# A two-layer diffusion block: mixers and the later units of a front are emitted in step with the expert gathers, with their VectorE work kept behind the dots

## The chip, the cores and the metric

The kernel runs on one core of a Trainium2 chip. The metric is the device time of one execution in microseconds (us); the median of three runs of the kernel before is 2957.38 us (2956.25 to 2957.57). The engines are TensorE (PE: matmuls; PEld: its weight loads), VectorE (DVE), ScalarE (ACT), GpSimd (POOL) and SyncE (SP). SP issues the plain transfers of the program in one queue, POOL the gathers.

## The reference, cut to what matters

Two streams of 256 tokens, the latent `x` and the context `ctx`, go through two layers. A layer has a mixer (attention and a bidirectional delta rule, the latent one reading the context's keys and states) and an expert layer (PEER): per token 8 heads pick 16 experts each out of 16384, by the top 16 of two lists of 128 keys and the top 16 of their sums. The context's expert layer is left out in the last layer.

```
x = x + g1 * mixer(rmsnorm(x, norm1_w) * (1 + sc1) + sh1, ctx...)
h = rmsnorm(x, norm2_w) * (1 + sc2) + sh2
q = (h @ wq);  s = q . subkeys;  sv, si = top_k(s, 16)          # the front
top_s, pos = top_k(sv[0] + sv[1], 16);  gate = softmax(top_s)
u = peer_u[expert];  act = gelu(sum(u * h))                    # a gather and a dot
x = x + g2 * sum(gate * act * peer_v[expert])
```

## The kernel before

A tile framework records instructions in the order in which the Python code emits them and then orders them itself: a scheduler plays the program with its own cost model and places each instruction on its engine when, in that play, it can run; emission order is its priority. On the chip each engine then runs its list strictly in order. Pools of tiles (`bufs` buffers a tag) make an instruction wait until a buffer's last reader is done.

The stages follow in `build` (L1063): the context's mixer of layer 0, `peer_start` and `peer_end` for it (expert layer 1, 0 by stream and layer), the latent mixer of layer 0 and its expert layer (0, 0), the context's mixer of layer 1 (keys and states only), the latent mixer of layer 1, and its expert layer (0, 1). The mixer of (0, 0) reads nothing of the context's expert layer, so the scheduler may run it beside those gathers; likewise the mixer of (1, 1) reads the context's result and runs beside the gathers of (0, 0). The latent mixer of layer 1 needs the last result of (0, 0) and has no gathers beside it.

An expert layer begins with its front (`peer_front`, L801): the norm to `h2`, transposes to `h2T`, eight heads of `wq` products (`ps_pq`), scores `sc`, and then `topk` (L888) in units. `CUTS` cuts the eight heads of the first 128 tokens (t=0) in units of 1, 2, 2 and 3 heads and those of the second 128 (t=1) in two units of 4. A unit ends with its list of indices `idx`. With `hl` (expert layers (1, 0) and (0, 1)) the front's products are made of three products of float32r halves (`product`, L150; a weight is split by ScalarE into `whi` and by VectorE into `wlo`, L127 and L128); without it each is one f32 product (L154).

`experts` (L1000) yields once per gather, 256 to an expert layer, 768 in all: POOL issues an indirect DMA of 1 MB into a buffer `G` (`gather`, L984); VectorE makes the dot `junk<-G,h2r` (L1024, with a small instruction that reads the sum); ScalarE makes `dg` (L1028, L1029); TensorE multiplies the second half of `G` into `acc` (L1033), which frees the buffer for a later gather. `h2r` are four copies of rows of `h2`, written by DMAs on SP (`replicated`), with one buffer each, so those for t=1 wait for the last dots of t=0. There are 7 gather buffers, 8 from the second half of expert layer (1, 0) on, and again 7 and then 14 in the last expert layer. `peer_start` emits the front's unit i+1, then the dots of unit i; the units of t=1 are emitted in step with the last unit of t=0, and `peer_end` runs the rest.

Of the kernel before, what the change touches and what calls it, by code (L numbers as in the profile page):

```python
# [38 lines left out]

QUADS = 4  # L40
QP = P // QUADS
QD = D // QUADS
GATHERS = 7
MORE_GATHERS = (1, 7)
# [7 lines left out]
def _blk(i, n):  # L52
    return slice(i * n, (i + 1) * n)
# [39 lines left out]

class Net:
    def __init__(self, tc, ap, out):
        self.tc, self.nc, self.ap, self.out = tc, tc.nc, ap, out

# [13 lines left out]
    def rsqrt(self, pool, x, n, mul, eps, tag):  # L111

        v = self.nc.vector
# [12 lines left out]
    def split(self, x, hi, lo):  # L126
        self.nc.scalar.copy(hi, x)  # L127
        self.nc.vector.tensor_tensor(lo, x, hi, op=ALU.subtract)  # L128
# [12 lines left out]
    def weight(self, name, l, i, hl, pool=None):  # L141
# [5 lines left out]
        lo = self.hlpool.tile([P, D], F32R, tag="wlo", name="wlo", bufs=self.lo_bufs)  # L147
# [29 lines left out]
    def late_constants(self, pool):  # L177
# [7 lines left out]
        with self.pool("clev_f") as cf:  # L185
            lf = cf.tile([P, 14, P], F32, name="clevf")
            nc.sync.dma_start(lf, ap["k_levels"].rearrange("m p n -> p m n"))
            nc.vector.tensor_copy(lv, lf)
# [40 lines left out]
    def modulation(self, l, pr, chunks):  # L229
# [7 lines left out]
        for n in chunks:  # L237
# [15 lines left out]
            nc.vector.tensor_tensor(  # L253
# [5 lines left out]
    def scale_columns(self, pr, i):  # L259

        for s in range(2):
            self.nc.vector.scalar_tensor_tensor(
# [21 lines left out]
    def rms_scale(self, pool, ss, n, tag):  # L284

        tot = pool.tile([P, n], F32, tag=tag + "_tot", name="tot")
        self.nc.vector.tensor_tensor(tot, ss[:, 0:n], ss[:, n : 2 * n], op=ALU.add)
        return self.rsqrt(pool, tot, n, 1.0 / D, EPS, tag)

    def norm1(self, pool, s, pr, hl):  # L290
# [3 lines left out]
        with self.pool(f"n1{s}") as pn:  # L294
            ss = pn.tile([P, 2 * NT], F32, name="n1ss")
            xn = []
            for t in range(NT):
# [4 lines left out]
                nc.vector.tensor_scalar_mul(xt, x[t], rs)  # L302
                xn.append(xt)
            for g in range(KB // 2):
# [4 lines left out]
                for j in range(2):  # L309
                    kb = 2 * g + j  # L310
                    a, b = pr["acol"][:, s, 0, kb : kb + 1], pr["mod"][:, s, kb : kb + 1]
                    if hl:
# [3 lines left out]
                        nc.vector.tensor_copy(hi, f)  # L316
                        nc.vector.tensor_tensor(lo, f, hi, op=ALU.subtract)
                    elif j == 0:
                        nc.vector.tensor_scalar(h[0][:, kb, :], ps[:, _blk(j, T)], a, b, op0=ALU.mult, op1=ALU.add)
# [25 lines left out]
    def attn_proj(self, pool, h, s, l, need_q, hl):  # L345
# [8 lines left out]
        def use_kv(t, ps):  # L354
            nc.scalar.copy(_flat(raw[t][:, NH:, :]), ps[:, :256])
            nc.vector.tensor_copy(_flat(vv[:, t]), ps[:, 256:])
# [6 lines left out]
    def attention(self, pool, raw, vv, pr, s, need_q, mixT):  # L363

        nc, v = self.nc, self.nc.vector
# [80 lines left out]
    def dn_project(self, pool, h, pr, l, blocks, qk, vtok, hl):  # L446

        nc, v = self.nc, self.nc.vector
# [21 lines left out]
    def dn_gates(self, pool, h, pr, l, g, beta, hl):  # L470

        nc, v = self.nc, self.nc.vector
# [3 lines left out]
        if hl:  # L476
            hi = self.hlpool.tile([P, D], F32R, tag="whi", name="whi")
            lo = self.hlpool.tile([P, D], F32R, tag="wlo", name="wlo", bufs=self.lo_bufs)
# [39 lines left out]
    def dn_norm(self, pool, qk, first, ktok, qT, kT):  # L518

        nc, v = self.nc, self.nc.vector  # L520
# [28 lines left out]
    def dn_chunk(self, pool, dn, t, d, it):  # L549
# [6 lines left out]
        nc, v = self.nc, self.nc.vector  # L556
# [89 lines left out]
    def dn_step(self, pool, it, vtok, d, S, O, first_o, new_S):  # L646

        nc, v = self.nc, self.nc.vector
# [53 lines left out]
    def dn_output(self, pool, O, gate, pr, mixT):  # L702
        nc, v = self.nc, self.nc.vector
# [19 lines left out]
    def mixer(self, s, l, pr, big, filler=(), rate=1, late_mods=(), late_consts=None):  # L723

        nc, v, hl = self.nc, self.nc.vector, big
# [75 lines left out]
    def peer_front(self, s, l, pr, hl, cuts):  # L801

        nc, v, ap = self.nc, self.nc.vector, self.ap
# [3 lines left out]
        with ExitStack() as st:  # L807
            pt = st.enter_context(self.pool("pt" + nm))
            hT = self.operand(pt, [P, KB, T], "h2T", hl)
            with self.pool("pn" + nm) as pn:  # L810
                A2 = self.broadcast_rows(pn, pr["acol"][:, s, 1, :], "A2")
                SH2 = self.broadcast_rows(pn, pr["mod"][:, s, 24:32], "SH2")

                h2.append(self.gbuffer()[:, :D] if hl else pt.tile([P, D], F32, name="h2"))
# [466 lines left out]
```

## Time and profile before

| | |
|---|---|
| median of three runs | 2957.38 us |
| the profiled execution | 2954.79 us |
| its span | 2952.7 us |
| TensorE busy | 1891.7 us (64%) |
| VectorE busy | 1866.0 us (63%) |
| ScalarE busy | 1094.0 us (37%) |
| GpSimd busy | 915.8 us (31%) |
| DMA, mean over the span | 326 GB/s |

No engine is near its full span. The stages have to be looked at one by one: by the granted clock, the DMA share (mean busy share of the 16 DMA engines) and the rate of the dots. A dot is counted in the views as two instructions of L1024. Dot k below is the k-th of the 768; dots 1 to 256 belong to expert layer (1, 0), 257 to 512 to (0, 0) and 513 to 768 to (0, 1).

### The profile page before, as it was taken

The page shows a single profiled execution, that of the slowest core. Times are in us where ns is not written, and L with a number is a line of the kernel's source. Part 1 is how long each engine was busy: PE and PEld are TensorE (multiplying, and loading weights), DVE is VectorE, ACT ScalarE, POOL GpSimd, SP SyncE. Part 2 cuts the span into 40 slices and gives each one's busy share as a digit, 9 for nine tenths or more (in the row PEclk, how much of TensorE's full clock was granted, in tenths as well). Part 3 has the DMA queues.
Part 4 walks back from the last instruction along what each step waited for, and adds up shares of the span by engine and source line. Part 5 has one row for each costly group of instructions (what it writes and reads, how often), then busy time and mean ns, then how long its engine had stood idle before and what let it go on. Part 6 is the DMA issues. An engine that isn't in the chain of part 4 may idle for free. (4 is left out here: it accounts for less than half of the span.)

```text
span 2952.7 us, 38689 instructions
## 1 busy us (share of the span) xinstructions
PE 1891.7 (64%) x13184; PEld 1085.0 (37%) x13184; DVE 1866.0 (63%) x4942; ACT 1094.0 (37%) x2609; POOL 915.8 (31%) x772
## 2 busy tenths in 40 slices
PE   7998836876888834458774444488988344444444
PEld 5876713533654611124550000077767110010001
DVE  5854798756775895446774444487557964455454
ACT  4533434745442432236442222254234322222222
POOL 0000234233343334332443444200002444435552
PEclk9999956997989955568985555599989555555555
DMA  7234899988999989999999999831358899999997
GB/s 277 100 121 168 290 342 354 348 359 326 339 370 374 416 303 394 394 418 367 366 352 372 420 420 419 359 115 44 115 193 319 315 378 419 420 375 420 420 419 308
DMA packets 163314, 961.64 MB, mean 326 GB/s; under 512 B 20784, under 2 KB 28336, under 8 KB 64816
## 3 DMA queue, kind: packets, MB, share of 16 engines
q0 software_dynamic: 110592, 805.36, 68.7%
q1 hardware_dynamic: 52528, 153.83, 15.0%
q8 instruction: 106, 1.74, 0.2%
q14 instruction: 88, 0.72, 0.1%
HBM read 945.48 MB, written 1.05 MB: 321 GB/s over the span
## 5 line engine op out<-in xcount | busy, mean ns | idle before, releaser
L988 POOL DMA_INDIRECT G<-in_peer_uv,idx x768 | 915.6, 1192 | 2001.7 <-PE acc L1033 762.3
L1024 DVE CUSTOM_DVE_ANT_0 junk<-G,h2r 128x1024 bf16<-128x1024 f32 x768 | 937.1, 1220 | 576.1 <-DMA G<-in_peer_uv,idx 554.6
L1033 PE MATMUL acc<-G,dg 128*32 128x256 f32 x6144 | 720.1, 558 | 889.8 <-ACT dg L1029 886.9
L1028 ACT ACTIVATE dg<-cident,act 128x32 f32<-128x32 f32 x768 | 246.7, 321 | 1158.9 <-DVE act L1024 1133.6
L1033 PEld LDWEIGHTS acc<-G,dg 128*32 128x32 f32 x6144 | 147.8, 130 | 1401.8 <-ACT dg L1029 1353.4
L1029 ACT ACTIVATE dg<-dg,pgate 128x32 f32<-128x32 f32 x768 | 246.6, 321 | 23.3
L128 DVE TENSOR_TENSOR wlo<-w,whi 128x1024 fp32r<-128x1024 f32 (+1 forms) x98 | 117.5, 1202 | 53.3 <-ACT whi L127 52.9
L127 ACT CAST whi<-w 128x1024 fp32r<-128x1024 f32 (+1 forms) x98 | 100.9, 1032 | 123.4 <-PE ps_pr L158 36.4
L621 PE MATMUL ps_P<-M,B 128*128 128x128 f32 x768 | 116.3, 299 | 33.7 <-DVE M L630 21.5
L621 PEld LDWEIGHTS ps_P<-M,B 128*128 128x128 f32 x768 | 101.3, 205 | 67.8 <-issue 35.0
L628 DVE COPY_PREDICATED X<-clev,ps_X 128x512 f32<-128x512 int8 x96 | 69.8, 727 | 73.6 <-PE ps_X L627 73.6
L627 PE MATMUL ps_X<-X,Pm 128*128 128x128 f32 x768 | 104.1, 281 | 1.5 <-ACT Pm L623 1.4
L623 ACT COPY Pm<-ps_P 128x512 f32<-128x512 f32 x96 | 56.2, 586 | 125.0 <-PE ps_P L621 124.2
L627 PEld LDWEIGHTS ps_X<-X,Pm 128*128 128x128 f32 x768 | 94.3, 194 | 16.5 <-issue 8.8
L244 PE MATMUL ps_ada<-w,silc 128*32 128x512 f32 x384 | 78.0, 666 | 10.2 <-DMA w<-in_ada_t 10.0
L462 DVE SCALAR_TENSOR_TENSOR cy<-craw,cw,cy 128x256 f32<-128x256 f32 x176 | 81.3, 481 | 2.0
L154 PE MATMUL ps_dn<-hT,w 128*128 128x256 f32 x320 | 81.2, 409 | 0.0
L1028 ACT ACT_TABLE_LOAD x57 | 73.1, 1283 | 14.3 <-DVE act L1024 13.3
L158 PE MATMUL ps_pq<-h2T_hi,wlo 128*128 128x256 f32 x256 | 75.4, 294 | 4.5 <-DVE wlo L128 4.4
L156 PE MATMUL ps_pq<-h2T_hi,whi 128*128 128x256 f32 x256 | 74.6, 291 | 0.6 <-ACT whi L127 0.6
L157 PE MATMUL ps_pq<-h2T_lo,whi 128*128 128x256 f32 x256 | 74.1, 290 | 0.0
L154 PEld LDWEIGHTS ps_dn<-hT,w 128*128 128x128 f32 x320 | 63.9, 206 | 16.5 <-issue 7.4
(316 smaller groups left out, 3081.2 us busy)
## 6 DMA issues: line engine op xcount, KB each, us to landing
w<-in_ada_t SPq DMA_DIRECT2D x96, 512.0 KB, 5.5
w<-in_wq_t SPq DMA_DIRECT2D x48, 512.0 KB, 5.3
w<-in_in_dn SPq DMA_DIRECT2D x44, 512.0 KB, 6.9
w<-in_in_rows SPq DMA_DIRECT2D x40, 512.0 KB, 4.0
w<-in_out_t SPq DMA_DIRECT2D x24, 512.0 KB, 5.3
G<-in_peer_uv,idx POOLq DMA_INDIRECT x768, 14.2
h2r<-h SPq DMA_DIRECT2D x64, 128.0 KB, 10.4
h2r<-G SPq DMA_DIRECT2D x32, 128.0 KB, 2.4
```

Of the source, the lines that this page charges most:

```text
L127: self.nc.scalar.copy(hi, x)
L128: self.nc.vector.tensor_tensor(lo, x, hi, op=ALU.subtract)
L154: self.nc.tensor.matmul(out, lhs[0], rhs[0], start=first, stop=last)
L244: nc.tensor.matmul(ps[_blk(g, 32), :], self.silc[:, kb, :], w[:, _blk(k, CW)], start=(kb < 4), stop=(kb >= 4))
L462: v.scalar_tensor_tensor(y, raw[:, k : k + T], cw[:, blk, k : k + 1], y, op0=ALU.mult, op1=ALU.add)
L621: nc.tensor.matmul(pp[:, _blk(h, P)], B[:, h, :], M[:, h, :], start=True, stop=True)
L627: nc.tensor.matmul(xp[:, _blk(h, P)], Pm[:, h, :], X[:, h, :], start=True, stop=True)
L988: self.nc.gpsimd.indirect_dma_start(out=G, out_offset=None, in_=self.ap[f"peer_uv{l}"], in_offset=bass.IndirectOffsetOnAxis(ap=idx, axis=0))
L1024: v.tensor_tensor_reduce(self.junk, G[:, :D], un["h2r"][j], scale=1.0, scalar=0.0, op0=ALU.mult, op1=ALU.add, accum_out=a)
L1028: nc.scalar.activation(dg, self.ident4, AF.Gelu, scale=a)
L1029: nc.scalar.mul(dg, dg, un["gate"][:, m, j : j + 1])
L1033: nc.tensor.matmul(self.acc[_blk((j + q) % QUADS, QP), _blk(q, QD)], dg, G[:, D + QD * q : D + QD * q + QD], start=(un["first"] and m == 0 ...
```

## The change

A class `Paced` stands in for the VectorE engine everywhere but in the dots' own units. It holds a queue of `experts` generators. While a pace is set, each VectorE instruction that a mixer or a front emits adds 0.1 + elements/960 to a counter, and at each full `pace` the next gather, dot and product of the queue are emitted right there. With `pin`, the VectorE instruction emitted after such a step is kept behind it in program order (`keep_in_program_order`), so the scheduler can't move it ahead of that dot.

`peer` replaces `peer_start` and `peer_end`: the first two units of a front are emitted without steps, the later ones at a pace of 1.0; pinned in (0, 0) and (0, 1), not in (1, 0). What is left in the queue is emitted in step with the mixer that follows, at a pace of 1.0 (mixer (0, 0)) and 0.7 (mixer (1, 1)), pinned, or drained at the end. All fronts use f32 products, and `h2` of t=0 has a tile of its own instead of a gather buffer. There are 8 gather buffers from the start of each group, and 14 for what is left after the last front.

```
-GATHERS = 7
-MORE_GATHERS = (1, 7)
+FRONT_PACE = 1.0
+MIXER_PACE = (1.0, 0.7)
+GATHERS = 8
+MORE_GATHERS = 6
...
+class Paced:
+    def step(self):
+        while self.queue:
+            self.inside = True
+            done = next(self.queue[0], self) is self
+            self.inside = False
+            if not done:
+                return True
+            self.queue.pop(0)
+        return False
...
+        def paced(*args, **kw):
+            ins = op(*args, **kw)
+            if self.inside or not self.pace:
+                return ins
+            if self.behind and self.pin:
+                self.tc.keep_in_program_order(ins)
+            self.behind = False
+            sizes = [math.prod(a.shape[1:]) for a in args if hasattr(a, "shape")]
+            self.due += 0.1 + max(sizes) / 960.0
+            while self.due >= self.pace:
+                self.due -= self.pace
+                self.behind |= self.step()
+            return ins
...
-    def peer_front(self, s, l, pr, hl, cuts):
+    def peer_front(self, s, l, pr, cuts):
...
-                    w = self.weight("wq_t", l, 2 * h + j, hl)
+                    (w,) = self.weight("wq_t", l, 2 * h + j, False)
...
+    def peer(self, s, l, pr, pin):
         cuts = [[(sum(u[:i]), n) for i, n in enumerate(u)] for u in CUTS]
+        self.dve.set()
+        for i, un in enumerate(self.peer_front(s, l, pr, cuts)):
+            self.dve.queue.append(self.experts(s, l, un))
+            if i == 1:
+                self.dve.set(FRONT_PACE, pin)
+        self.dve.set()
...
+                    self.peer(1, 0, prs[0], False)
                 with ExitStack() as st:
                     psums(st, 3, 3)
+                    self.dve.set(MIXER_PACE[0], True)
                     self.mixer(0, 0, prs[0], False)
-                    units = self.peer_start(0, 0, prs[0], False)
-                self.peer_end(0, 0, units)
+                    self.peer(0, 0, prs[0], True)
                 with ExitStack() as st:
                     psums(st, 3, 3)
                     _run(params[1])
+                    self.dve.set(MIXER_PACE[1], True)
                     _run(mods(1, range(0, 4), 0))
                     self.mixer(1, 1, prs[1], False)
+                    self.dve.set()
+                self.dve.drain()
```

How the built programs differ is read from the order of the instructions on an engine. All engines' lists are the same up to the end of the context's first mixer. First place: VectorE in the first unit of the first front, (1, 0), from the splits of its weights to the one-hot products `oh`; before:

```order
L128 TENSOR_TENSOR wlo<-w,whi 128x1024 x3
L910 MAX sv<-sc_2709 128x8 x2
...
L128 TENSOR_TENSOR wlo<-w,whi 128x1024
L910 MAX top<-cand 128x8
...
L963 TENSOR_TENSOR ge<-top 128x16
L128 TENSOR_TENSOR wlo<-w,whi 128x1024
L932 TENSOR_SCALAR r<-pos 128x16
...
L950 TENSOR_TENSOR oh<-ab,ciota 128x256 x2
L128 TENSOR_TENSOR wlo<-w,whi 128x1024
```

And now, where every VectorE instruction has the wrapper's line, L131:

```order
L131 CAST ciota<-ciotaf 128x1024
L131 MAX sv<-sc_2701 128x8 x2
...
L131 MAX top<-cand 128x8
...
L131 TENSOR_TENSOR ge<-top 128x16
L131 TENSOR_SCALAR r<-pos 128x16
...
L131 TENSOR_TENSOR oh<-ab,ciota 128x256 x2
```

The splits of the weights are gone from between the steps of the unit. Second place: VectorE where the mixer of (0, 0) makes its first normalised row `xn`. Before, it follows dot 45, and the fronts' last units have just passed:

```order
L981 CAST idx<-ps_ig 32x64
...
L1024 ISA junk,act<-G,h2r 128x1024
L1024 ISA act 128x1
L120 TENSOR_TENSOR n_t<-n_y 128x1
...
L302 TENSOR_SCALAR xn_6670<-res_x_79,n_y 128x1024
...
L1024 ISA junk,act<-G,h2r 128x1024
L1024 ISA act 128x1
L302 TENSOR_SCALAR xn_6692<-res_x_80,n_y 128x1024
```

Now it follows dot 85, and between dots 42 and 85 VectorE has nothing but dots:

```order
L131 ISA junk,act<-G,h2r 128x1024
L131 ISA act 128x1
L131 ISA junk,act<-G,h2r 128x1024
L131 ISA act 128x1
L131 SCALAR_TENSOR_TENSOR n_t<-n_t,n_a 128x1
L131 SCALAR_TENSOR_TENSOR n_y<-n_t,n_y 128x1
L131 TENSOR_SCALAR xn_4555<-res_x_79,n_y 128x1024
```

So this mixer starts 40 dots later. Its last row of `h` comes after dot 228 instead of 177. Of the next front's index lists `idx`, the four of t=0 come after dots 239 to 263 instead of 188 to 221, and the two of t=1 after dots 277 and 303 instead of 256 and 272 (where the maxima and one-hots for them were through by dot 228). The mixer of (1, 1) has its scan (`ps_P`) beside dots 360 to 412 instead of 328 to 360. Third place: TensorE where the front of (0, 0) begins, after its transposes `ps_h`. Before, products of the front and of the dots alternate:

```order
L154 MATMUL ps_pq<-h2T,w 128x256 x12
L1033 MATMUL acc<-G,dg 32x256 x4
L154 MATMUL ps_pq<-h2T,w 128x256 x4
L1033 MATMUL acc<-G,dg 32x256 x4
L154 MATMUL ps_pq<-h2T,w 128x256 x13
...
L154 MATMUL ps_pq<-h2T,w 128x256 x3
L1033 MATMUL acc<-G,dg 32x256 x16
L854 MATMUL ps_sc<-skT,pqT 128x128 x4
```

Now they stand in blocks (four products of L1084 are one dot's):

```order
L899 MATMUL ps_pq<-h2T,w 128x256 x32
L1084 MATMUL acc<-G,dg 32x256 x28
L907 MATMUL ps_sc<-skT,pqT 128x128 x4
L1084 MATMUL acc<-G,dg 32x256 x4
L899 MATMUL ps_pq<-h2T,w 128x256 x28
L1024 MATMUL ps_ig<-ig,crep 128x32 x4
L907 MATMUL ps_sc<-skT,pqT 128x128 x8
L899 MATMUL ps_pq<-h2T,w 128x256 x4
L1084 MATMUL acc<-G,dg 32x256 x28
```

So up to 32 products of the front are ahead of the products that free the buffers of seven dots. In the attention of mixer (0, 0) the dots move a little as well: it has eight passes of a maximum `am`, an exponent on ScalarE and a reciprocal `asm` on VectorE, and a dot stands between the last two in five of the eight, where it was one. After dot 256, at the change of expert layers, 65 VectorE instructions of the front now stand before dot 257, where there were 8. ScalarE's list has 133 loads of function tables where it had 127.

## Rows read from the trace of the kernel before

**Rows 1.** The page, DMA queues: packets, MB, time as share of 16 engines' span.

```profile
q0 software_dynamic: 110592, 805.36, 68.7%
```

**Rows 2.** Stretches, L1024 alone: length, VectorE busy (x instructions), PE clock, DMA share, GB/s.

```profile
334.00:485.00 151.00, 52.75 (x87) 0.64 0.91 343
485.00:935.00 450.00, 163.73 (x268) 0.88 0.92 353
935.00:1095.00 160.00, 53.63 (x87) 0.79 0.93 370
1095.00:1190.00 95.00, 43.27 (x72) 0.57 1.00 377
1337.00:1543.00 206.00, 78.47 (x129) 0.90 0.94 357
1671.00:1871.00 200.00, 98.54 (x160) 0.50 1.01 419
2245.00:2392.00 147.00, 52.38 (x85) 0.63 0.90 339
```

**Rows 3.** Stretches, all: length, PE, PEld, DVE, ACT, POOL, clock, DMA share, GB/s.

```profile
0.00:334.00 334.00, 291.76 (x1926) 236.10 (x1927) 205.84 (x539) 140.15 (x249) 0.27 (x5) 0.94 0.50 171
334.00:485.00 151.00, 76.28 (x574) 42.06 (x576) 138.70 (x620) 59.39 (x156) 65.81 (x49) 0.64 0.91 343
485.00:935.00 450.00, 357.54 (x2361) 216.53 (x2353) 303.37 (x663) 223.43 (x484) 162.93 (x137) 0.88 0.92 353
935.00:1095.00 160.00, 109.16 (x711) 71.41 (x710) 135.88 (x629) 57.26 (x156) 49.73 (x44) 0.79 0.93 370
2245.00:2392.00 147.00, 75.61 (x563) 41.41 (x562) 137.43 (x610) 57.68 (x147) 61.93 (x49) 0.63 0.90 339
```

**Rows 4.** Waits of POOL, 485 to 935 us: us in total, times, longest.

```profile
POOL G L988 <- PE acc L1033: 137.7, 57, 12.2
```

**Rows 5.** Waits of DVE in the same stretch.

```profile
DVE asm L429 <- ACT ap L428: 16.8, 8, 2.4
DVE junk L1024 <- DMA G<-in_peer_uv,idx: 15.1, 9, 2.6
```

**Rows 6.** Timeline of DVE, attention of mixer (0, 0): start, us, instruction [idle before].

```profile
700.72 0.15 DVE L427 TENSOR_SCALAR am<-am 128x1 f32<-128x1 f32 x1
703.28 0.16 DVE L429 RECIPROCAL asm<-asm 128x1 f32<-128x1 f32 x1 [2.42 <-ACT ap L428]
703.40 1.23 DVE L1024 CUSTOM_DVE_ANT_0 junk<-G,h2r 128x1024 bf16<-128x1024 f32 x1
```

**Rows 7.** Timeline of DVE, first unit of the first front: its first and last step.

```profile
313.54 0.48 DVE L910 MAX8 sv<-sc 128x8 f32<-128x128 f32 x2
...
326.35 0.18 DVE L960 SCALAR_TENSOR_TENSOR ig<-oh 128x16 f32<-128x16 bf16 x1
```

**Rows 8.** Groups of DVE, 313.5 to 330.5 us: busy us, mean ns | idle before.

```profile
L128 DVE TENSOR_TENSOR wlo<-w,whi 128x1024 fp32r<-128x1024 f32 x6 | 7.4, 1225 | 3.4 <-ACT whi L127 3.4
```

**Rows 9.** Timeline of PE, first front: float32r halves, three products to a block.

```profile
302.84 0.28 PE L158 MATMUL ps_pq<-h2T_hi,wlo 128*128 128x256 f32 x1
...
303.20 0.28 PE L158 MATMUL ps_pq<-h2T_hi,wlo 128*128 128x256 f32 x1
```

**Rows 10.** Timeline of PE, front of (0, 0): f32, one product to a block.

```profile
937.61 5.35 PE L154 MATMUL ps_pq<-h2T,w 128*128 128x256 f32 x24
```

**Rows 11.** Timeline of POOL: the first gather of (1, 0).

```profile
333.93 1.08 POOL L988 DMA_INDIRECT G<-in_peer_uv,idx  x1 [333.48 <-DVE sv L910]
```

**Rows 12.** The same view: the first gather of (0, 1).

```profile
2244.96 0.94 POOL L988 DMA_INDIRECT G<-in_peer_uv,idx  x1 [348.66 <-DVE sv L910]
```

**Rows 13.** Timeline of DVE: between dot 256 and dot 257.

```profile
1178.90 0.08 DVE L1024 DVE_READ_ACCUMULATOR2_ANT act<- 128x1 f32 x1
...
1190.74 1.22 DVE L1024 CUSTOM_DVE_ANT_0 junk<-G,h2r 128x1024 bf16<-128x1024 f32 x1
```

**Rows 14.** The page, groups: busy us, mean ns | idle before.

```profile
L1028 ACT ACT_TABLE_LOAD x57 | 73.1, 1283 | 14.3 <-DVE act L1024 13.3
```

More of the change, by code (lines that the diff above doesn't have):

```diff
@@ L91, in _zip, with __init__, set, drain @@
         yield
+class Paced:
+    def __init__(self, tc):
+        self.tc, self.vector = tc, tc.nc.vector
+        self.queue, self.pace, self.pin = [], 0.0, False
+        self.due, self.behind, self.inside = 0.0, False, False
+    def set(self, pace=0.0, pin=False):
+        self.pace, self.pin, self.due = pace, pin, 0.0
+    def step(self):
[7 more added lines that the diff above has]
+        return False
+    def drain(self):
+        while self.step():
+            pass
+    def __getattr__(self, name):
+        op = getattr(self.vector, name)
+        def paced(*args, **kw):
[11 more added lines that the diff above has]
+            return ins
+        return paced
 class Net:
@@ L843, in head @@
                 for j in range(2):
-                    w = self.weight("wq_t", l, 2 * h + j, hl)
+                    (w,) = self.weight("wq_t", l, 2 * h + j, False)
                     for kb in range(KB):
-                        self.product(
-                            ps[:, _blk(j, T)], [a[:, _blk(kb, P)] for a in w], [a[:, kb, :] for a in hT], kb == 0, kb == KB - 1
+                        nc.tensor.matmul(
+                            ps[:, _blk(j, T)], w[:, _blk(kb, P)], hT[:, kb, :], start=(kb == 0), stop=(kb == KB - 1)
                         )
@@ L858, in head @@
                     nc.scalar.copy(_flat(sc[t][:, 2 * h : 2 * h + 2, :]), ps[:, _blk(t, T)])
-            for h0, n in cuts[0]:
+            for i, (h0, n) in enumerate(cuts[0]):
                 tk = self.topk(pool, sc[0], h0, n)
@@ L1058, in experts @@
                 v.tensor_tensor(xs, xs, out, op=ALU.add)
-    def peer_start(self, s, l, pr, hl):
+    def peer(self, s, l, pr, pin):
         cuts = [[(sum(u[:i]), n) for i, n in enumerate(u)] for u in CUTS]
-        front = self.peer_front(s, l, pr, hl, cuts)
-        n0 = len(cuts[0])
-        units = [next(front)]
-        def rest():
-            for un in front:
-                if un is not None:
-                    units.append(un)
-                for _ in range(5):
-                    yield
-        for i in range(n0):
-            if i + 1 < n0:
-                units.append(next(front))
-            _run(self.experts(s, l, units[i]), rest() if i == n0 - 1 else None)
-        return units
-    def peer_end(self, s, l, units):
-        for un in units[len(CUTS[0]) :]:
-            _run(self.experts(s, l, un))
+        self.dve.set()
[4 more added lines that the diff above has]
+        self.dve.set()
     def build(self):
@@ L1173, in build @@
                     psums(st, 3, 3)
-                    self.hlpool = pool("hl3", 2, st)
-                    self.lo_bufs = 2
-                    units = self.peer_start(0, 1, prs[1], True)
-                self.more_gathers(ga, MORE_GATHERS[1])
-                self.peer_end(0, 1, units)
+                    self.peer(0, 1, prs[1], True)
+                self.more_gathers(ga, MORE_GATHERS)
+                self.dve.drain()
             for t in range(NT):
```

64 lines of the change are left out of this document (28 added, 36 removed).

## The prediction

> **What bounds the kernel now.** I read the page's table of queues first. The gathers move 805 MB, 768 of 1 MB [rows 1]. Then I cut the span at its stages and counted dots, two instructions to a dot [rows 2]. Where no front or mixer runs beside them (1671 to 1871 us) 80 dots take 200 us, 2.50 us each, at a DMA share of 1.01: there the transfers are the limit. 768 of them make 1920 us. The first stage (334 us) and the latent mixer of layer 1 have no gathers beside them and are not touched before their last few us. What the change can win is the difference between 2.50 us and the pace beside fronts and mixers [rows 2]: 3.47 us a dot in the first front (43.5 dots in 151 us), 3.36 in mixer (0, 0) (134 in 450), 3.68 in the front of (0, 0) (43.5 in 160), 3.19 in mixer (1, 1) (64.5 in 206), 3.46 in the last front (42.5 in 147).
>
> Two causes are to be seen. In the fronts VectorE is the limit: busy 138.7 of 151, 135.9 of 160 and 137.4 of 147 us [rows 3]. In mixer (0, 0) VectorE is busy 303 of 450 us, yet a dot waits for its gather for 15 us in all [rows 5], while POOL waits 138 us for the products that free a buffer [rows 4]. So the dots stand in line behind a mixer's instruction that waits for another engine. One case: a reciprocal waits 2.42 us for the exponent, and the dot behind it, ready or not, starts only then [rows 6].
>
> Part of that difference is no loss: the mixers' weights use the same DMA engines. In the first 334 us a share of 0.50 moved 171 GB/s [rows 3], that is 167 us for 57 MB, some 1.5 us for a weight of 0.52 MB. The 48 weights of mixer (0, 0) and the front behind it are thus worth 73 us. From 485 to 1190 us there are 213.5 dots [rows 2]: 534 + 73 = 607 us of transfers in 705 us.
>
> **The change part by part.**
>
> *Fronts in f32.* A block of 256 columns starts every 0.36 us with halves (302.84 to 303.20 us [rows 9]) and every 0.22 us in f32 (24 in 5.35 us [rows 10]), both with other work out of the way. The 128 products of a front fall from 46 to 28 us of TensorE, the two weights ahead of the first unit from 5.8 to 3.5 us. The 16 splits go too, 1.225 us of VectorE each [rows 8]. Four of them stand inside the first unit, between 313.54 and 326.35 us [rows 7], so it shrinks by 5 us. The first gather [rows 11, 12] should come 2.3 + 5 us earlier, and as the index product also waits behind fewer products I take 8 us; with only TensorE's part it is 2, with all the splits of that stretch (7.4 us and 3.4 us of waits [rows 8]) 13. In two fronts: **-16 us** (-4 to -26).
>
> The Trainium skill (FP8 and Floating Point Precision, TensorE Precision Notes) says that a true FP32 product takes four passes. With 0.12 us for each product of halves that would be 0.48 us against 0.36, the first two weights 2 us later instead of 2.3 earlier, and this term -8 instead of -16. The rows show 0.22 us, less than two such products, so I go by them.
>
> *First front, the rest.* The eight splits left after the first gather take 10 us of a VectorE that is full: 151 us become 141. An eighth buffer adds nothing while VectorE is the limit. Then dots 43 to 85 have VectorE for themselves: 41.5 at 2.50 are 104 us, where the mixer's pace made 139. Dot 85 comes 245 us after the first gather instead of 290: 45 us ahead.
>
> *Mixer (0, 0) and its front.* This is where the 45 us are paid back. The mixer's own work is unchanged and starts 40 dots later. I take its 450 us, plus nine more dots (143 for 134) at 1.22 us on VectorE, minus the four further waits of 2.4 us that a dot now fills [rows 5, 6]: 451. The 28 dots from 228 to 256 run at the pace of the front, 3.68: 103. Two blocks of about 30 f32 products (7 us each) now stand ahead of products that free buffers: 14. The change of layers costs 12 us as before (1178.90 to 1190.74 us [rows 13]), and the 65 front instructions behind dot 256 another 11 (the first unit's 12.8 us less its splits is 8 us for some 45, or 0.17 us each). Sum: 245 + 451 + 103 + 14 + 12 + 11 = 836 us to dot 257; before it was 1190 - 334 = 856. **-20 us** (-100 at 2.50 us a dot plus weights; +55 if every dot from 85 to 256 ran at 3.68).
>
> Here the pin adds waits: a mixer instruction now can't pass a dot that is still in flight, and behind it wait the mixer's next products and, through SP's four weight buffers, its loads. That costs nothing while the mixer has dots to spare; before, the front of (0, 0) was through by dot 228, 28 ahead of its use, and now the list of its first unit is ready at dot 239, with the buffer for gather 257 free at dot 249.
>
> *Dots 257 to 512.* What is left of the front (t=1) lies beside dots 257 to 303, which the transfers pace: some 100 us of VectorE in 118. Mixer (1, 1) is spread over 112 dots instead of 91. Of that stage's 28 weights (16 of modulations, 8 and 4 of projections) I put 22 into its stretch: it loses 206 - 64.5 x 2.50 - 22 x 1.5 = 12 us now. **-10 us** (-30 to +10).
>
> *Last front.* Splits out (13 us of a full VectorE) and its last units moved beside later dots, so the transfers pace it: 42.5 x 2.50 = 106, ten weights 15, 2 MB of row copies 6, together 127 for 147 at best. **-10 us** (-21 to 0).
>
> Six more table loads at 1.28 us [rows 14] lie on a ScalarE that is half idle: nothing, or 8 us if each delayed a dot's product. All bytes moved are the same.
>
> Sum: -16 - 20 - 10 - 10 = -56 us against the profiled execution's 2954.8 us (span 2952.7 and 2.1 around it): 2898.8. It lies 2.6 us under the median of the runs, so 2901 us is the prediction.
>
> **The rivals.**
>
> *The transfers alone pace everything.* If dots put ahead of the mixers keep all eight buffers in flight, dots 85 to 257 take 171 x 2.50 + 73 + 10 = 510 us instead of 591, 81 us less. With -30 and -20 for the later terms the sum is -16 - 101 - 30 - 20 = -167: 2790 us. For it: dots hardly wait for gathers now, so there is room. Against it: in the mixers VectorE's list still holds instructions that wait for TensorE and ScalarE, a dot behind each. Half way there is 2845.
>
> *Won early, given back late.* The mixer's chain costs what it cost, and the front of (0, 0), crowded into 28 dots, eats the whole lead. For it: a DMA share of 0.92 and 0.93 there leaves 50 us of idle DMA at most in 610 [rows 2]. Only the two first gathers and the last front remain: -26, 2931 us.
>
> *Slower: the mixer's late start.* After 42 pure dots the granted clock is at 0.50, the 1.2 GHz level [rows 2], and the mixer resumes from there; if it and its front then hold each of the 171 dots at 3.68 us, that is 629 us for 85 to 256 instead of 554, and the sum is +19: 2976. It turns slower than before from 3.57 us a dot on (610 us). For it: 3.68 is measured in the one stretch that is as crowded as dots 228 to 263 will be. Against it: the mixer is less dense than it was.
>
> *No change:* the leads of the fronts and a dearer mixer cancel, within 0.2% (6 us, about what a measurement can tell from none).
>
> **How the numbers follow.** My forecast has 0.5, with a range of its own of 2875 to 2925; transfers alone 0.12; won and given back 0.2; no change 0.06; slower 0.12. The first three are faster by over 0.2%: 0.82; same 0.06, slower 0.12. The range of 2840 to 2955 leaves out the better half of the first rival and the slower case, some 0.18.
>
> **What would show it.** First gathers near 326 and 2237 minus what was won before; dot 85 about 245 us behind the first gather with 2.50 us a dot from 43 on; 3.2 us a dot or less in mixer (0, 0); and from dot 228 to 263 the slowest stretch. Products `ps_pq` every 0.22 us in all fronts. I would be wrong if dots wait for gathers through the whole mixer (then the first rival), or if dot 257 comes later than 856 us behind the first gather (then the third).

## Result and profile after

The changed kernel takes 2889.13 us (median; 2884.98 to 2890.75) against 2956.82 us of the kernel before beside it, a ratio of 0.9772 [0.9755, 0.9789]. The profiled execution has 2888.39 us with a span of 2886.6: 66.1 us less span.

In the changed kernel every VectorE instruction passes through the paced helper and has its line, L131; the views go by tiles. First `junk` by stretch: length, VectorE busy (x dots; the small read of the sum is not counted here), TensorE clock, DMA share, GB/s.

```profile
332.00:490.00 158.00, 58.51 (x48) 0.67 0.92 360
490.00:570.00 80.00, 39.21 (x32) 0.50 1.01 420
580.00:1048.00 468.00, 174.47 (x144) 0.88 0.95 363
1048.00:1164.00 116.00, 35.01 (x30) 0.88 1.00 387
1164.00:1283.00 119.00, 58.24 (x49) 0.52 1.00 401
1650.00:1850.00 200.00, 97.97 (x80) 0.50 1.01 420
2198.00:2338.00 140.00, 59.59 (x49) 0.67 1.00 413
```

Against [rows 2] there are three changes: a stretch of bare dots (490 to 570 us, 2.50 us each) between the first front and its mixer; transfers that no longer stand still beside the front of (0, 0) (share 1.00, where 935 to 1095 us had 0.93); and a last front paced by its transfers (2.86 us a dot, share 1.00 for 0.90). Mixer (0, 0) still takes 3.25 us a dot. All engines in five of these stretches, with columns as in [rows 3]:

```profile
332.00:490.00 158.00, 87.61 (x589) 46.09 (x592) 140.60 (x635) 60.11 (x165) 65.60 (x55) 0.67 0.92 360
490.00:570.00 80.00, 34.53 (x256) 6.38 (x256) 39.47 (x64) 20.53 (x64) 35.21 (x32) 0.50 1.01 420
580.00:1048.00 468.00, 365.80 (x2430) 217.03 (x2430) 312.51 (x664) 225.88 (x497) 172.24 (x145) 0.88 0.95 363
1048.00:1164.00 116.00, 94.53 (x632) 72.26 (x632) 92.83 (x418) 46.29 (x122) 31.10 (x29) 0.88 1.00 387
2198.00:2338.00 140.00, 85.84 (x581) 43.88 (x579) 123.46 (x502) 50.83 (x145) 63.88 (x56) 0.67 1.00 413
```

In mixer (0, 0) the waits have not gone. Waits from 580 to 1048 us, one of POOL's and two of VectorE's (us in total, times, longest), against [rows 4, 5]:

```profile
POOL G L1039 <- PE acc L1084: 169.2, 70, 25.1
...
DVE junk L131 <- DMA G<-in_peer_uv,idx: 19.7, 14, 3.4
...
DVE asm L131 <- ACT ap L482: 12.2, 8, 2.4
```

The starts of single dots in the two traces, in us from the span's start, and the lead of the new kernel (before less after):

| dot | before | after | lead |
|---|---|---|---|
| first gather | 333.9 | 331.6 | 2.3 |
| 33 | 454.7 | 455.0 | -0.3 |
| 85 | 634.8 | 580.7 | 54.1 |
| 228 | 1110.9 | 1047.3 | 63.6 |
| 257 | 1190.7 | 1163.6 | 27.1 |
| 305 | 1337.1 | 1282.8 | 54.3 |
| 512 | 1911.7 | 1866.3 | 45.4 |
| gather of dot 513 | 2245.0 | 2198.6 | 46.4 |
| 577 | 2459.0 | 2375.4 | 83.6 |
| 768 | 2935.7 | 2870.9 | 64.8 |

The fronts' products did not come out as forecast. TensorE from the first front's first product to its first list, time, length, instruction (xcount of records):

```profile
300.57 13.82 PE L899 MATMUL ps_pq<-h2T,w 128*128 128x256 f32 x62
314.23 1.05 PE L907 MATMUL ps_sc<-skT,pqT 128*128 128x128 f32 x8
315.12 12.68 PE L899 MATMUL ps_pq<-h2T,w 128*128 128x256 f32 x58
327.64 0.97 PE L1024 MATMUL ps_ig<-ig,crep 128*128 128x32 f32 x8
```

The same stretch of VectorE, the two instructions ahead of which it waits longest (time, length, instruction, idle before and its end):

```profile
315.77 0.49 DVE L131 MAX8 sv<-sc 128x8 f32<-128x128 f32 x2 [16.37 <-ACT sc L911]
...
328.65 0.16 DVE L131 CAST idx<-ps_ig 32x16 int32<-32x16 f32 x1 [5.17 <-PE ps_ig L1024]
```

POOL's first gather, against [rows 11]:

```profile
331.64 1.07 POOL L1039 DMA_INDIRECT G<-in_peer_uv,idx  x1 [331.19 <-DVE sc L131]
```

A head has 16 products, and the 62 records ahead of the first score product stand for 31 of the 32 products of two heads. The page says the same of the whole program: three fronts of 128 products give 768 records.

```profile
L899 PE MATMUL ps_pq<-h2T,w 128*128 128x256 f32 x768 | 181.0, 396 | 0.0
```

So the trace has two records for one f32 product of 256 columns, and a block costs 13.82 / 31 = 0.45 us. The sorts from score to list fell from 12.8 us [rows 7] to 7.5 (315.77 to 323.31 us), but VectorE waits 16.4 us ahead of them and 5.2 behind. In the kernel before, too, the first list's product stood behind the front's products on TensorE:

```profile
329.17 0.97 PE L973 MATMUL ps_ig<-ig,crep 128*128 128x32 f32 x8
```

TensorE is busy without a gap from the front's first product to this one in both kernels: 26.7 us before (302.50 to 329.17), 27.1 us now (300.57 to 327.64).

### The profile page after: what moved, and what is told of

Its sections match the earlier page's. It is cut to its first block, busy times and chain, and to the rows that moved or that the text cites. A ratio compares the mean times of both kernels' runs of the same rounds, so it can differ in the third digit from the quotient of the medians.

```text
span 2886.6 us, 37977 instructions
## 1 busy us (share of the span) xinstructions
PE 1888.9 (65%) x12928; PEld 1089.0 (38%) x12928; DVE 1837.9 (64%) x4902; ACT 1066.9 (37%) x2583; POOL 918.4 (32%) x772
## 3 DMA queue, kind: packets, MB, share of 16 engines
HBM read 945.48 MB, written 1.05 MB: 328 GB/s over the span
## 4 chain that ended last, share of the span: by engine, by line
DMA 40%; PE 30%; DVE 18%; ACT 6%; issue 4%; POOL 1%; SPq 0%; POOLq 0%; DVEq 0%; ACTq 0%
DMA G<-in_peer_uv,idx 35%; DVE junk L131 6%; PE ps_pq L899 4%; PE acc L1084 3%; DMA h2r<-h 2%; PE ps_P L675 2%; PE ps_dn L208 2%; PE ps_pr L208 2%; PE ps_X L681 2%; PE ps_ada L298 1%; PE ps_pr L211 1%; PE ps_pr L210 1%; PE ps_pr L212 1%; DVE si L131 1%; DMA w<-in_ada_t 1%
## 5 line engine op out<-in xcount | busy, mean ns | idle before, releaser
L131 DVE CUSTOM_DVE_ANT_0 junk<-G,h2r 128x1024 bf16<-128x1024 f32 x768 | 937.3, 1220 | 511.0 <-DMA G<-in_peer_uv,idx 496.7
L1084 PE MATMUL acc<-G,dg 128*32 128x256 f32 x6144 | 704.9, 550 | 826.5 <-ACT dg L1080 823.2
L1084 PEld LDWEIGHTS acc<-G,dg 128*32 128x32 f32 x6144 | 148.7, 129 | 1321.2 <-ACT dg L1080 1275.8
L899 PE MATMUL ps_pq<-h2T,w 128*128 128x256 f32 x768 | 181.0, 396 | 0.0
L899 PEld LDWEIGHTS ps_pq<-h2T,w 128*128 128x128 f32 x768 | 151.0, 200 | 28.2 <-issue 7.4
L131 DVE COPY_PREDICATED X<-clev,ps_X 128x512 f32<-128x512 int8 x96 | 69.7, 728 | 72.6 <-PE ps_X L681 72.6
L131 DVE TENSOR_TENSOR wlo<-w,whi 128x1024 fp32r<-128x1024 f32 (+1 forms) x66 | 78.7, 1194 | 36.7 <-ACT whi L181 36.7
L181 ACT CAST whi<-w 128x1024 fp32r<-128x1024 f32 (+1 forms) x66 | 67.3, 1023 | 71.6 <-PE ps_pr L212 36.3
L131 DVE SCALAR_TENSOR_TENSOR cy<-craw,cw,cy 128x256 f32<-128x256 f32 x176 | 81.1, 482 | 1.6
L131 DVE MAX8 sv<-sc 128x8 f32<-128x128 f32 x192 | 47.5, 283 | 39.6 <-ACT sc L911 38.7
## 6 DMA issues: line engine op xcount, KB each, us to landing
G<-in_peer_uv,idx POOLq DMA_INDIRECT x768, 16.4
```

What stands on the lines that cost most here:

```text
L131: ins = op(*args, **kw)
L899: nc.tensor.matmul(ps[:, _blk(j, T)], w[:, _blk(kb, P)], hT[:, kb, :], start=(kb == 0), stop=(kb == KB - 1))
L1084: nc.tensor.matmul(self.acc[_blk((j + q) % QUADS, QP), _blk(q, QD)], dg, G[:, D + QD * q : D + QD * q + QD], start=(un["first"] and m == 0 ...
```

## Experiments

The theories are A, the place of VectorE's other work among the dots; B, the shorter fronts; C, the eighth buffer; further ones where they came up. Leads are against the kernel before.

**f32 alone** (kernel before)

```
...
-                    units = self.peer_start(1, 0, prs[0], True)
+                    units = self.peer_start(1, 0, prs[0], False)
...
-                    units = self.peer_start(0, 1, prs[1], True)
+                    units = self.peer_start(0, 1, prs[1], False)
```

> The kernel before, with one part of the change: both of its split fronts, (1,0) and (0,1), multiply in f32; seven gather buffers, the units' and mixers' places in the code as before. Theory A (the gain of 68 us comes from where VectorE's other work stands among the dots, and the f32 products alone buy next to nothing): the time stays within 2945 to 2968 us, the first gather goes out at 331 to 335 us, and the dots of the last front come no earlier than 5 us against their first. Theory B (the gain comes from the shorter fronts, 38.8 us of split work less on VectorE): 2900 to 2925 us, with the dots after the first front's first 64 earlier by 20 us or more. Theory C (the eighth buffer carries it): 2950 to 2960 us, as under A, and it is the next kernels that tell A from C.

Measured 2949.84 us, 0.998 [0.9971, 0.9989]. The first gather goes out at 331.0 us, the second group's at 2239.6 (lead 5.4), and the lead at dot 768 is 5.5. A holds: f32 fronts alone, on the kernel before, are worth 6 us of 68. What they are worth inside the changed kernel no run shows.

**The pin left out**

```
-            if self.behind and self.pin:
-                self.tc.keep_in_program_order(ins)
```

> The changed kernel with its pin left out: the paced helper still emits the mixers' and later units' instructions between the dots, but nothing holds an instruction behind the dot it follows, so on VectorE the first mixer's first instructions stand behind dot 32 again instead of dot 80, and the second front's sorts behind dots 176 to 223 in one lump instead of 224 to 303. f32 fronts and eight buffers stay. Theory A (place among the dots): most of the gain goes, 2930 to 2960 us, and dots 48 to 80 no longer run at 39.9 us for 16. Theory B (f32 fronts) and theory C (eighth buffer): 2885 to 2905 us, since both of their causes are still in it.

Measured 2933.31 us, 0.9929 [0.9918, 0.9941]. Some 44 us went with two lines. Dots 49 to 81 take 106.8 us (79.8 in the changed kernel), and the last front is slow again: 49 dots need 168 us instead of 140, with VectorE busy 140.62 of them and the DMA share at 0.95 instead of 1.00.

```profile
2230.00:2398.00 168.00, 87.80 (x594) 45.59 (x592) 140.62 (x630) 57.41 (x157) 70.43 (x61) 0.66 0.95 369
```

A holds. What the other 22 us are made of, beside the 6 of f32, was not taken apart.

**Mixers out of step**

```
-                    self.dve.set(MIXER_PACE[0], True)
+                    self.dve.drain()
...
-                    self.dve.set(MIXER_PACE[1], True)
+                    self.dve.drain()
```

> The changed kernel with the mixers out of step: in front of each of the two mixers, all dots still in the queue are emitted, and the mixer's code stands behind them as in the kernel before (its instructions are then pulled forward among the dots, the first mixer's from dot 32 on); the fronts stay paced and pinned, and second front's sorts stand behind dots 176 to 207 and 256 to 335. Theory A: the mixers' share of the gain goes (dots 85 to 228 in 467 us after, 54 us ahead of before at dot 85), the last front's lead of some 20 us stays: 2905 to 2940 us. Theory B and theory C: 2880 to 2900 us.

Measured 2903.45 us, 0.9819 [0.9805, 0.9834]: 14 us lost, just short of A's range, too much for B and C. The lead is 12.3 us at dot 81 (50.6), yet 34.0 at dot 257 (27.1) and 81.7 at dot 337 (57.5); it falls to 25.6 at dot 433, where the second mixer lies. So the 50 us that the changed kernel is ahead at dot 81, by the first mixer's later start, are not what it keeps at dot 257.

**Fronts out of step**

```
-        for i, un in enumerate(self.peer_front(s, l, pr, cuts)):
-            self.dve.queue.append(self.experts(s, l, un))
-            if i == 1:
-                self.dve.set(FRONT_PACE, pin)
-        self.dve.set()
+        front = self.peer_front(s, l, pr, cuts)
+        n0 = len(cuts[0])
+        units = [next(front)]
+        self.dve.drain()
...
+        for i in range(n0):
+            if i + 1 < n0:
+                units.append(next(front))
+            _run(self.experts(s, l, units[i]), rest() if i == n0 - 1 else None)
+        self.dve.queue += [self.experts(s, l, un) for un in units[n0:]]
```

> The changed kernel with the fronts out of step: each front's units are emitted as in the kernel before (unit i+1, then the dots of unit i, the second tile's unit beside the last unit of the first tile), and only the second tile's dots are left in the queue for the mixers, which stay paced and pinned; the first mixer then begins behind dot 128 and the second front's sorts stand behind dots 256 to 287. f32 fronts and eight buffers stay. Theory A: the fronts' share goes, the mixers' stays: 2900 to 2945 us, the last front's lead against before at its end falls from 20 us to within 8 us. Theory B and theory C: 2880 to 2905 us.

Measured 2954.18 us, 0.9997 [0.9987, 1.0006]: the whole gain is gone, which is more than A gave it. Its dots 1 to 256 are through at 1105.6 us, 72.2 ahead of before; then the end of the mixer and, from 1153.1 us on, the front of (0, 0) have no dots left beside them, and dot 257 starts at 1191.5, 0.7 late. The edit takes the fronts' pin away with their step. The stretch between, all engines:

```profile
1105.00:1192.00 87.00, 80.17 (x360) 56.21 (x361) 34.70 (x149) 20.66 (x47) 5.47 (x6) 0.93 0.49 149
```

Half the DMA time is unused for 87 us. The row shows why a lead inside a group is no gain by itself: the dots run ahead are missing beside the mixer's end and the next front.

**Seven buffers**

```
-GATHERS = 8
-MORE_GATHERS = 6
+GATHERS = 7
+MORE_GATHERS = (1, 7)
...
+                self.more_gathers(ga, MORE_GATHERS[0])
...
-                self.more_gathers(ga, MORE_GATHERS)
+                self.more_gathers(ga, MORE_GATHERS[1])
```

> The changed kernel with the gather buffers of the kernel before: seven during the first front, one more behind it, one and then seven more in the last group; f32 fronts, paced helper and pin as changed. After the earlier runs, theory A is that the gain is the place of VectorE's other work among the dots, held by the pin (44 of 66 us went with the pin, all of it with the fronts put back in a lump); the eighth buffer only widens the cover at the places where VectorE is called away for long: 2889 to 2902 us. Theory C (the eighth buffer carries a good part of the gain; the rival): 2910 to 2935 us.

Measured 2892.41 us, 0.9783 [0.9768, 0.9798] beside 0.9772 [0.9755, 0.9789]: no difference that can be told. C falls.

**TensorE's order in the fronts.** `behind` is an order edge without a wait.

```
-                        nc.tensor.matmul(
+                        mm = nc.tensor.matmul(
...
+                        if h and self.last_sc is not None:
+                            self.behind(mm, self.last_sc)
+                        if h == 2:
+                            self.behind(mm, self.last_ig)
...
```

> The changed kernel with one thing added, the order of TensorE in the fronts: the products of head h+1 stand behind the score products of head h, and those of head 2 behind the first unit's index replication; nothing else changes. In the changed kernel 31 f32 products of two heads stand in front of the first score product, and VectorE waits 16.4 us for the first scores and 5.2 us for the replicated indices. Theory D (the f32 products, at two records of 0.216 us each, are what held the first gathers at 331.6 and 2198.6 us instead of the 326 forecast; TensorE's order is the wait): the first gather comes 5 to 9 us earlier in each front, 2872 to 2884 us in all. Theory E (the wait only moves: the first unit's sorts then wait for their own scores or for the weights' transfers, or the dots give it back): 2885 to 2893 us.

Measured 2889.8 us, 0.9775 [0.9762, 0.9789]. The edit did what it should: one head, its scores, the next head, the first list's product. TensorE's timeline:

```profile
299.32 7.77 PE L900 MATMUL ps_pq<-h2T,w 128*128 128x256 f32 x32
307.76 1.16 PE L912 MATMUL ps_sc<-skT,pqT 128*128 128x128 f32 x8 [0.68 <-ACT pqT L908]
308.76 7.07 PE L900 MATMUL ps_pq<-h2T,w 128*128 128x256 f32 x32
317.17 1.08 PE L1035 MATMUL ps_ig<-ig,crep 128*128 128x32 f32 x8 [1.34 <-DVE ig L131]
```

Its first gather on POOL:

```profile
321.28 1.07 POOL L1050 DMA_INDIRECT G<-in_peer_uv,idx  x1 [320.83 <-DVE sc L131]
```

The first gather comes 10.3 us earlier, that of the last group 10.1. So the first half of theory D holds: what held the first gather was what stood ahead of it on TensorE (32 products here, 60 in the changed kernel, at the same price). Its time does not: nothing of the 10 us is left, dot 33 starts at 454.2 us (455.0 in the changed kernel), dot 529 at 2257.2 (2256.1), and the time is theory E's. From 400 to 490 us VectorE is nearly full, as it is in the changed kernel (83.40 of 90 us); all engines, this kernel:

```profile
400.00:490.00 90.00, 34.02 (x251) 11.77 (x248) 84.80 (x387) 32.58 (x91) 34.34 (x28) 0.56 0.85 316
```

But the order also makes the rest of the front later. The last products of the first front, in the changed kernel and then in this one:

```profile
379.35 4.15 PE L899 MATMUL ps_pq<-h2T,w 128*128 128x256 f32 x18
...
394.65 4.58 PE L900 MATMUL ps_pq<-h2T,w 128*128 128x256 f32 x20
```

They end some 16 us later. So the run does not tell what an early first gather is worth by itself; one that leaves the front's end where it was has not been tried.

**Only the second mixer in step** (the first of the two `drain` edits alone)

> The changed kernel with only the first mixer out of step (in front of it, the rest of the first front's dots is emitted), the second mixer and the fronts paced and pinned. With both mixers out of step the dots stood 81.7 us ahead of the kernel before at dot 337 (57.5 in the changed kernel) and only 25.6 at dot 433, where the second mixer stood in a lump. Theory A (each stretch's cost is set by how VectorE's other work lies among its dots): the lead at dot 337 stays at 78 to 85 us, of what was lost to dot 433 at least half is kept, 2855 to 2885 us. Theory F (what is won early is given back: at the end of the second front's dots the lead is near 45 whatever stands before): 2886 to 2905 us.

Measured 2911.49 us, 0.9848 [0.9832, 0.9863]. Neither theory's range has it. The lead is 83.8 us at dot 337, as A said, and 31.7 at dot 433, against 25.6 with both mixers out of step: the step kept 6 us of the 56 lost there, not half. At dot 512, with the second mixer behind both kernels, these are gone too (a lead of 29.1 us against 29.4). Six more were lost between dots 512 and 513 (345.9 us for 339.7), with nothing edited there; why is open. In all the kernel is 8 us slower than with both mixers out of step (0.9848 [0.9832, 0.9863] for 0.9819 [0.9805, 0.9834]): behind a first mixer out of step, the second one's step is worth nothing. No run takes the step from the second mixer alone.

**Both of the last two**

> The last two kernels in one: TensorE's order in the fronts, and the first mixer out of step. If their gains are of different stretches (theories A and D), they add up: 2840 to 2876 us. If either gives back what the other wins (E or F), 2880 to 2900 us.

Measured 2909.32 us, 0.9848 [0.9831, 0.9865]: the same time as without TensorE's order, and outside both ranges. The early gather is given back here too.

**The first front pinned**

```
-                    self.peer(1, 0, prs[0], False)
+                    self.peer(1, 0, prs[0], True)
```

> The changed kernel with the first front pinned too (the only part of the changed kernel that was paced without the pin): on VectorE 657 and 89 other instructions stand ahead of dots 1 to 16 and among dots 16 to 31 instead of 709 and 189. Theory A (place among the dots decides; the pinned last front runs its first 64 dots in 169 us, the unpinned first front in 192): dots 1 to 65 take 168 to 178 us, 10 to 22 us are kept to the end, 2866 to 2880 us. Theory E (what is won before dot 33 is given back, as the 10 us of the earlier first gather were): dot 33 again at 454 to 456 us, 2885 to 2895 us.

Measured 2871.18 us, 0.9709 [0.9693, 0.9726]: 18 us faster than the changed kernel from one word. The first gather is where it was (331.6 us); dot 33 starts at 429.3, and from dot 81 to dot 512 the lead over the changed kernel stays within 16 to 22 us. The first front of this kernel, all engines:

```profile
332.00:400.00 68.00, 52.40 (x345) 35.69 (x343) 56.51 (x247) 27.59 (x74) 30.72 (x27) 0.85 1.00 408
400.00:490.00 90.00, 39.90 (x292) 8.88 (x288) 79.25 (x275) 29.35 (x84) 41.14 (x36) 0.50 1.01 420
490.00:570.00 80.00, 37.63 (x271) 10.48 (x275) 65.42 (x208) 27.97 (x85) 34.23 (x32) 0.52 1.01 419
```

The middle stretch in the changed kernel (its row from 490 to 570 us stands above):

```profile
400.00:490.00 90.00, 38.62 (x284) 11.77 (x280) 83.40 (x343) 34.88 (x97) 38.86 (x32) 0.54 0.86 326
```

The pin moves front work out of the 90 us in which VectorE was nearly full into the bare 80 us behind them (208 VectorE instructions there instead of 64), and the DMA share is 1.0 throughout. E, whose time held for TensorE's order, falls for this.

**Pinned, with TensorE's order**

> The kernel of the run before this one, with TensorE's order in the fronts added. If VectorE's backlog of front work (busy 59.4 of the 60 us from 420 to 480 us) was what gave the earlier first gather back, then with the pin the 10 us are worth something in the first front: 4 to 10 us less than the kernel before it. If the gathers are given back in any case, the two are within 4 us of each other.

Measured 2868.11 us, 0.9696 [0.968, 0.9712], 3.1 us below the kernel before it with intervals that overlap. Dot 33 starts 5.4 us later than without the order, though the first gather goes out 8.6 earlier (323.0 us). TensorE's order buys nothing clear of noise in either form; here, too, it makes the front's last product later (400.5 us for 378.4).

**Denser mixers** (on the pinned kernel)

```
-MIXER_PACE = (1.0, 0.7)
+MIXER_PACE = (1.4, 1.0)
```

> The kernel with the first front pinned, and the mixers paced to a dot after every 1.4 and 1.0 us of their own VectorE work instead of 1.0 and 0.7: the first mixer then uses up fewer dots, more are left beside the second front, and the second front's own dots are left to fewer mixer instructions each. Theory A says that a stretch costs what its VectorE chain takes when its dots no longer fit beside it: if the first mixer's 467 us are its own chain with a dot pinned between, it gets shorter with fewer dots in it and dot 257 comes 5 to 20 us earlier, 2851 to 2868 us. The rival (the mixer's time is its waits for TensorE and ScalarE, and the dots beside it are free): the fewer dots are missing from cover, the gathers stand still more, dot 257 comes no earlier, and the time is 2868 to 2890 us.

Measured 2919.69 us, 0.9874 [0.9843, 0.9904], 48 us slower. The rival has the direction, and the size is beyond it. This kernel from about dot 97 to dots 225, 257 and 337, all engines:

```profile
597.00:1044.00 447.00, 364.47 (x2383) 232.71 (x2380) 294.06 (x641) 208.98 (x463) 143.57 (x128) 0.89 0.93 349
1044.00:1173.00 129.00, 71.87 (x499) 44.49 (x497) 118.51 (x586) 44.81 (x122) 40.15 (x33) 0.72 0.90 335
1173.00:1428.00 255.00, 168.60 (x1114) 85.87 (x1114) 155.03 (x363) 111.92 (x260) 87.87 (x80) 0.74 0.97 388
```

The pinned kernel between the same dots:

```profile
597.00:1015.00 418.00, 326.83 (x2186) 196.35 (x2179) 275.70 (x560) 199.66 (x438) 151.21 (x127) 0.89 0.94 358
1015.00:1145.00 130.00, 103.19 (x698) 74.27 (x696) 101.39 (x435) 50.85 (x135) 36.08 (x34) 0.88 1.00 384
1145.00:1372.00 227.00, 120.15 (x844) 42.91 (x844) 157.97 (x491) 78.69 (x215) 93.87 (x80) 0.62 1.01 406
```

Unused DMA time: 31 + 13 + 8 = 52 us against 25 and none (length times one minus share). A's idea, that the mixer's own chain gets shorter, is seen: the mixer starts at 566 us in both, and the first product of the front behind it comes 25 us earlier, here and in the pinned kernel:

```profile
1006.67 4.07 PE L899 MATMUL ps_pq<-h2T,w 128*128 128x256 f32 x16
...
1032.22 7.99 PE L899 MATMUL ps_pq<-h2T,w 128*128 128x256 f32 x36
```

But only 215 dots had started by then, instead of 229. The others have to be made beside the front, and dot 257 comes 28 us later. At dot 512, with both mixers behind it, the kernel is 41 us behind the pinned one; how much of that is the second mixer's new pace was not taken apart.

**Thinner mixers** (on the pinned kernel)

```
-MIXER_PACE = (1.0, 0.7)
+MIXER_PACE = (0.9, 0.6)
```

> The kernel with the first front pinned, and the mixers paced thinner instead of denser: a dot after every 0.9 and 0.6 us of their own VectorE work instead of 1.0 and 0.7. Denser cost 48 us (2919.7), because the dots are what keeps transfers going beside the mixer's waits. Theory A': thinner goes on in that direction, 2850 to 2866 us, with the second mixer's stretch (dots 305 to 433, 385 us so far) shorter. Rival: the dots are rationed, what the first mixer uses up is missing beside the second front (124 and 207 other instructions stand among dots 240 to 255 and 256 to 271, against 165 and 178 so far), dot 257 comes 5 to 30 us later: 2872 to 2895 us.

Measured 2882.76 us, 0.9754 [0.9732, 0.9776], 12 us slower than with 1.0 and 0.7. The rival's time holds, by another road than it gave. Dot 257 comes 24 us earlier (1121.2 for 1145.1), not later; the next 16 dots take 72.8 us (43.1), with VectorE busy 55.5 of the 73 us and 0.84 of the DMA time used; what is left of the front now lies there:

```profile
1121.00:1194.00 73.00, 43.62 (x303) 28.73 (x301) 55.53 (x258) 22.87 (x61) 18.12 (x16) 0.78 0.84 309
```

So the 24 us won beside the first mixer are given back: dots used up beside a mixer are missing beside the front. At dot 512, with the front and both mixers behind it, this kernel is 4.6 us behind the pinned one, and 2.7 more go between dots 512 and 513. Both paces were changed at once, in this run and in the denser one, so neither gives a price for one pace alone; that the pair 1.0 and 0.7 is better than both is what they show.

## Why the prediction was right, and where it was not

The forecast was 2901 us, with a sum of -56; the spans differ by 66.1 us. The mechanism was right in the main: the gain lies in where VectorE's work stands among the dots. That the sum came so near is in part luck, since the first term lacked 13 us and the other three, priced at 40, gave 61.5. By its own terms:

1. *First gathers, -16: measured -2.3 and -1.0.* This is the step that failed. It took the 24 records of [rows 10] for 24 products, hence 0.22 us a block. They are two for each product; the f32 block is 0.45 us, dearer than three products of halves at 0.36 [rows 9]. The rule of the Trainium skill that was weighed there (FP8 and Floating Point Precision, TensorE Precision Notes: true FP32 takes four passes) had the right direction: an estimate of 0.48 by it. The path was wrong as well. The term priced two weights ahead of the first unit and VectorE's splits, but in both kernels the first list's product waits for all that stands ahead of it on TensorE, 26.7 us before and 27.1 now; the splits' 5 us were won beside that. With 32 products ahead of it instead of 60, at the same price, the first gather came 10.3 us earlier. Those 10 us won no time, in a kernel whose front ended later for it; what an early first gather is worth alone stays open.
2. *First front and mixer (0, 0), -20: measured -24.8 from first gather to dot 257.* Behind the first gather, dot 85 came after 249.0 us (forecast 245), dots 85 to 228 took 466.6 (451), and from 228 to 257 it was 116.3 (103 + 14 + 12 + 11 = 140). The sum of 832.0 for 836 is right by errors that cancel: the mixer was slower by 16, its front and change of layer faster by 24. The rate of that front was nearly as priced, 99.5 us for dots 228 to 256 (103 forecast), and dot 257 started 16.8 us behind dot 256 (12 + 11 forecast). What did not show is the 14 us for the two blocks of products. They were twice as long as priced (14.72 and 12.35 us), and POOL did wait behind the first:

```profile
1053.96 14.72 PE L899 MATMUL ps_pq<-h2T,w 128*128 128x256 f32 x64
...
1069.55 0.94 POOL L1039 DMA_INDIRECT G<-in_peer_uv,idx  x1 [17.88 <-PE acc L1084]
```

Yet transfers already under way and the front's own weights ran on meanwhile: the DMA share is 1.01 from 1050.7 to 1069.6 us, 0.83 of it the gathers' queue. "The mixer's chain costs what it cost" proved nearly true, POOL's waits for products included.
3. *Dots 257 to 512, -10: measured -18.3.* The first 48 dots ran at 2.48 us, as said (118 forecast, 119 measured), and won 27. Dots 305 to 433, where mixer (1, 1) now lies, took 384.9 us for 376.1 and lost 9. The two do not price the front and the mixer, since before the mixer's first products (`ps_ada`) came at dot 272 already and now at dot 303; only their sum compares like with like.
4. *Last front, -10: measured -18.4 from its first gather to dot 768.* 42 dots took 112.0 us (140.0 before), so transfers do pace it. The lead grew by 39 us to dot 577, and 22 of them were gone by dot 641; the gathers' issues had won less (gather 577 went out 182.6 us behind the group's first before, 158.8 after), since the kernel before let its transfers run on while its dots stood: dot 577 started 31.5 us behind its gather there, 18.0 now.
5. *Rivals.* Transfers alone did not come: mixer (0, 0) keeps 3.26 us a dot. Given back: true of the stretch 228 to 257, where the lead falls from 63.6 to 27.1, but not of all of it. The slower case did not come in the changed kernel; what comes nearest to it, a front left without dots, is seen with the fronts out of step, at 85.9 us between dots 256 and 257.

Of the signs that it gave, dot 85 came (249.0 us for 245). Dots 228 to 263 took 3.86 us each and were not the slowest: dots 97 to 132, inside mixer (0, 0), took 4.22. The mixer as a whole, at 3.26 us a dot, did not come down to 3.2, and a product every 0.22 us was not there.

What the experiments add is the cause's name: the fronts in step and the pin, not f32 by itself, not the buffer. The prediction spoke of the pin as a wait that costs nothing; it is what holds 44 us. The parts do not add up (fronts out of step 65 us, pin 44, the step of both mixers 14, that of the first alone 22), because each decides how many dots are left for the next.

## What to carry to other kernels

Where transfers are the limit, count the dots (or other work that frees a buffer) as cover to be rationed: a lead inside one group is worth only what is left of it beside the next crowded stretch, so read a change's gain behind that stretch. Emitting work in step is half the edit when a scheduler may pull it forward; the half that holds the place was worth more here (44 us of 66), and the one front left without it another 18 us (2871.18 us, the first front pinned). Before pricing an instruction by its records, divide the records of the whole page by the instructions that the code emits. Before pricing what a shorter chain wins, look for what stands ahead of its end on the other engine.

## What the runs showed of the hardware

One f32 product of 256 columns leaves two records of some 0.22 us; a block of them starts every 0.44 to 0.49 us (16 in 7.07 and 7.77 us at a granted clock of 0.98 from 300 to 320 us in the kernel with TensorE's order), so f32 was slower than three float32r products at 0.36 (granted clock 1.00 from 302.5 to 311.5 us in the kernel before). The f32 score products show the same: 8 records for 4 products, in 1.05 us.

In the stretches of bare dots the granted clock is 0.50, the 1.2 GHz level, with TensorE busy 34.5 of 80 us, and the dots still keep 2.50 us at a DMA share of 1.01: there the transfers are the limit, and the low clock does not show in the pace.
